# Opening of a two-layer hybrid backbone: all token loads in quarters, eight raw buffers, and the first key and query products queued behind the modulation blocks

## The chip, the cores and the metric

The kernel runs on one core of one Trainium2 chip. The metric is device time in microseconds of one execution of the whole program. Before the change three runs took 1936.62, 1938.57 and 1939.97 us; the median is 1938.57 us.

## The reference

Two consecutive layers of a bidirectional network on 256 latent tokens and 256 context tokens of width 1024, in float32. Only its opening matters here:

```
h_lat, h_ctx = x, ctx
ml = split(silu(c)     @ ada_w[l] + ada_b[l], 6)      # modulation of the latent tokens
mc = split(silu(c_ctx) @ ada_w[l] + ada_b[l], 6)      # modulation of the context tokens
xl = rmsnorm(h_lat, g) * (1 + ml[1]) + ml[0]
xc = rmsnorm(h_ctx, g) * (1 + mc[1]) + mc[0]
yl, yc = even_mixer(xl, xc, ...)                      # begins with xs @ w_in: keys, queries, values, gates
```

After the mixer come a dense SwiGLU, a second mixer and a mixture of eight experts.

## The kernel before, in words

Tokens lie transposed: `res` holds 128 partitions by 8 slabs `k` of 128 channels by 512 tokens (context first). Each float32 product is made of three: weights and tokens are split into a rounded part `hi` and a rest `lo`, and `mm3` (L232) adds hi by hi, hi by lo and lo by hi into one accumulator bank. ScalarE writes the `hi` parts and VectorE the `lo` parts (`hilo`, L634).

The opening, in `even_mixer` from L491 on, does four things.

1. `first_rstd` (L362) loads the tokens in two transfers, squares the eight slabs on ScalarE (L369), adds them on VectorE (L371), sums over partitions on TensorE (L374), takes the reciprocal root with small VectorE steps (L380 to L390) and spreads it over the partitions on TensorE (L398).
2. The modulation comes in blocks of 256 columns. A call of `ada` (L279) loads one block of 1 MB into a raw buffer, multiplies it on TensorE in eight matmuls of 32 by 256 (L286), copies the result to SBUF on VectorE (L289), turns it by two small matmuls (L292) and adds the bias on VectorE (L295). Blocks go in pairs, a scale block into bank `c0` and a shift block into bank `c1`; pair `j` serves the slabs 2j and 2j+1. "Turned" below means that L295 of a pair's second block has run.
3. For each slab VectorE scales the tokens (L506, tile `xm`), ScalarE applies the pair's scale and shift (L405, two instructions per slab, one for each half of the tokens), and `hilo` writes `xhi` and `xlo`.
4. The first products, of the key and query columns of `w_in`, run over the slabs into four banks at once (two called `mm`, one `pr`, one `o`): 3 matmuls of 128 by 512 for each bank and slab, 12 for a slab, 96 in all. Their two weight chunks are loaded in two transfers and split in halves of four slabs.

After them come the gate products (L667), the convolution of the four banks (`conv`, L437) and the delta rule.

Each engine executes its instructions in the order in which they stand, and each may wait on semaphores of the other engines. That order is set by the framework's list scheduler, which sees the whole program and starts from the order in which the code emits. Loads go through SyncE's one queue. Buffers of a pool are reused in turn, and a new load waits until the old content has been read. The raw pool of the opening has six buffers and the eight blocks pass through it; the weight chunks use a ring of their own with two.

Of the kernel before, what the change touches and what calls it, by code (L numbers as in the profile page):

```python
# [18 lines left out]
P = 128  # L19
D = 1024  # L20
KD = 8
# [141 lines left out]
class Kernel:  # L163
# [115 lines left out]
    def ada(self, l, blocks, tag, pool=None):  # L279
        nc = self.nc  # L280
        for b2 in blocks:
            w = self.load(self.I["ada"][b2], pool).rearrange("p (k c) -> p k c", k=KD)
            ps = self.bank(tag)
            for k in (0, 2, 4, 6, 1, 3, 5, 7):
                j = k // 2
                nc.tensor.matmul(ps[32 * j:32 * j + 32, :256], lhsT=self.sT[:, k], rhs=w[:, k],  # L286
                                 start=k % 2 == 0, stop=k % 2 == 1, tile_position=(0, 32 * j))
            part = self.small.tile([P, 256], F32, name="part", bufs=2)
            nc.vector.tensor_copy(part, ps[:, :256])  # L289
            pc = ps[:, 256:260]  # L290
            for i in range(2):
                nc.tensor.matmul(pc[:, 2 * i:2 * i + 2], lhsT=part[:, i * P:(i + 1) * P], rhs=self.cb["sel2"],  # L292
                                 start=True, stop=True)
            bias = self.par[f"ada_b{l}"][:, 2 * b2:2 * b2 + 2]
            nc.vector.tensor_tensor(self.vec[l][:, 2 * b2:2 * b2 + 2], pc.rearrange("p (i r) -> p i r", i=2),  # L295
                                    bias[:, :, None].to_broadcast([P, 2, 2]), op=ALU.add)
# [65 lines left out]
    def first_rstd(self, pool, tag, row):  # L362
        nc = self.nc
        acc = pool.tile([P, T], F32, name="sqacc")
        for i in range(2):
            nc.sync.dma_start(self.res[:, 4 * i:4 * i + 4], self.I["x"][:, 4 * i:4 * i + 4])
        for k in range(KD):
            sq = pool.tile([P, T], F32, tag="sq", name="sq", bufs=3) if k else acc
            nc.scalar.activation(sq, self.res[:, k], AF.Square)  # L369
            if k:  # L370
                nc.vector.tensor_tensor(acc, acc, sq, op=ALU.add)  # L371
        ps = self.bank(tag)
        for t in range(4):
            nc.tensor.matmul(ps[:, t:t + 1], lhsT=acc[:, t * P:t * P + P], rhs=self.mean_d[:, 0:1], start=True,  # L374
                             stop=True)
        return self.rstd_row(self.rstd_col(ps, 4), row)
# [80 lines left out]
    def even_mixer(self):  # L457
        nc, I = self.nc, self.I
        with ExitStack() as st:
# [27 lines left out]
            with ExitStack() as s1:  # L487
                xp = s1.enter_context(self.pool("x0"))
                x = self.pair(xp, "x")
                self.psum(s1, "ps_even", mm=2, pr0=1, pr1=1, c0=1, c1=1, o0=1, o1=1)  # L490
                with ExitStack() as s0:  # L491
                    raw = s0.enter_context(self.pool("raw0", 6))
                    wp = s0.enter_context(self.pool("work0"))
                    vecs = self.mod_vectors(0, 0)
                    banks = [self.bank(t) for t in ("mm", "mm", "pr1", "o1")]
                    rs = self.first_rstd(wp, "o0", "pr0")
                    ahead = []
                    for j in range(4):
                        for i in range(2):
                            self.ada(0, (4 + j - 4 * i,), f"c{i}", raw)  # L500
                            if j < 2 and i:
                                ahead.append(self.weights(I["w_in"][6 - 2 * j], KD))
                        self.mod_scale(vecs[0], 0, 0, slice(2 * j, 2 * j + 2))
                        for k in (2 * j, 2 * j + 1):
                            xm = wp.tile([P, T], F32, tag="xm", name="xm", bufs=3)
                            nc.vector.tensor_tensor(xm, self.res[:, k], rs, op=ALU.mult)  # L506
                            self.modulate_split(xm, k, vecs, x)
                        for k in ((), range(4), (4, 5), (6, 7))[j]:
                            for i, ps in enumerate(banks):
                                m = slice(i % 2 * P, i % 2 * P + P)  # L510
                                whi, wlo = ahead[i // 2]
                                self.mm3(ps, whi(k)[:, m], wlo(k)[:, m], x[0][:, k], x[1][:, k], k == 0, k == KD - 1)
# [80 lines left out]
            with ExitStack() as s3:  # L593
# [4 lines left out]
                raw = s3.enter_context(self.pool("raw1", 2))  # L598
# [1130 lines left out]
```

## Time and profile before

| | |
|---|---|
| median of three runs | 1938.57 us (1936.62 to 1939.97) |
| the profiled execution | 1935.74 us |
| its span, first to last instruction | 1933.9 us |
| granted TensorE clock, mean | 0.967 |
| busy: TensorE, VectorE, ScalarE | 91%, 75%, 52% of the span |

The profile is of one execution. Its span is 1.84 us shorter than its time, which is what lies around the first and last instruction, and its time is 2.83 us below the median. Times inside the trace count from the span's start. In rows of the timeline the first number is the start, the second how long the row lasts (several instructions merged), and the bracket says how long the engine had stood idle and what ended that. The granted clock is shown as a share of full speed: 1.00 is 2.4 GHz, 0.50 is 1.2 GHz. Before the first record of the clock, at 29.8 us, the column shows 1.00 whatever the clock was.

### The profile page before, as it was taken

To read this page: it belongs to the slowest core of one execution; us is meant where nothing else is said; L and a number is where in the kernel's file an instruction comes from. 1 tells how busy PE (TensorE), PEld (TensorE's weight loads), DVE (VectorE), ACT (ScalarE), POOL (GpSimd) and SP (SyncE) were. 2 spreads that over 40 slices of the span, in tenths; PEclk is the share of its full clock that TensorE was granted. 3 is DMA by queue.
4 is the path that set the end of the run, shared out by engine and by line. 5 is a ranking of instruction groups with operands and counts; after the bars stand their busy time and mean duration, and the time that the engine had idled before them with its cause. 6 is when DMAs were issued, how large, how long until landed. Compare 5 with 4: busy or idle time off the path is not lost.

```text
span 1933.9 us, 28843 instructions
## 1 busy us (share of the span) xinstructions
PE 1768.6 (91%) x11628; PEld 1390.4 (72%) x11628; DVE 1445.9 (75%) x1966; ACT 1006.3 (52%) x1131; POOL 90.3 (5%) x92
## 2 busy tenths in 40 slices
PE   6989999698999999989999879989999899998996
PEld 3657776377888888778876768777777677777775
DVE  4577888657995383456685678888888889888987
ACT  3433325635232222366562357776677677767774
POOL 0011102200000000002110000000000000000000
PEclk8999999798999999989999889999999999999997
DMA  7232111325666163123203339999999999989993
GB/s 291 91 111 88 46 42 49 109 88 200 236 238 239 66 223 125 66 80 109 87 23 146 144 133 359 363 344 363 345 341 363 353 346 341 370 335 360 352 380 119
DMA packets 57310, 409.32 MB, mean 212 GB/s; under 512 B 6480, under 2 KB 6864, under 8 KB 8016
## 3 DMA queue, kind: packets, MB, share of 16 engines
q1 hardware_dynamic: 57168, 407.39, 56.5%
q8 instruction: 93, 1.52, 0.3%
q14 instruction: 49, 0.40, 0.1%
HBM read 406.32 MB, written 1.05 MB: 211 GB/s over the span
## 4 chain that ended last, share of the span: by engine, by line
PE 71%; DVE 17%; ACT 7%; issue 4%; POOL 1%; DMA 0%; SPq 0%; DVEq 0%; ACTq 0%; POOLq 0%
DVE lo L636 10%; PE bank_gu L1604 6%; PE bank_b L234 6%; PE bank_b L235 6%; PE bank_b L236 6%; PE bank_gu L1603 5%; ACT hi L635 5%; PE bank_mm L234 4%; PE bank_mm L235 4%; PE bank_mm L236 4%; PE bank_gu L1606 3%; PE bank_dn L1660 3%; PE bank_dn L1659 2%; PE bank_dn L1662 1%; PE bank_tr L1619 1%
## 5 line engine op out<-in xcount | busy, mean ns | idle before, releaser
L636 DVE TENSOR_TENSOR lo<-raw,hi 128x2048 fp32r<-128x2048 f32 (+1 forms) x398 | 765.4, 1946 | 186.3 <-ACT hi L635 184.2
L635 ACT ACTIVATE hi<-raw 128x2048 fp32r<-128x2048 f32 (+1 forms) x398 | 641.3, 1632 | 276.0 <-PE bank_b L235 140.5
L1604 PE MATMUL bank_gu<-lo,xghi 128*128 128x512 f32 (+1 forms) x384 | 148.9, 388 | 27.2 <-DVE lo L636 26.7
L1604 PE MATMUL bank_gu<-lo,xs 128*128 128x512 f32 (+1 forms) x384 | 146.2, 387 | 7.5 <-DVE lo L636 6.4
L1603 PE MATMUL bank_gu<-hi,xghi 128*128 128x512 f32 (+1 forms) x384 | 145.6, 379 | 0.0
L1606 PE MATMUL bank_gu<-hi,xglo 128*128 128x512 f32 (+1 forms) x384 | 144.5, 376 | 0.0
L1603 PE MATMUL bank_gu<-hi,xs 128*128 128x512 f32 (+1 forms) x384 | 144.3, 382 | 0.2
L234 PE MATMUL bank_b<-xhi,hi 128*128 128x512 f32 x352 | 138.0, 394 | 2.9 <-ACT xhi L635 2.9
L234 PE MATMUL bank_mm<-xhi,hi 128*128 128x512 f32 (+1 forms) x320 | 120.9, 380 | 21.5 <-ACT hi L635 15.3
L235 PE MATMUL bank_b<-xlo,hi 128*128 128x512 f32 x352 | 137.9, 392 | 0.0
L236 PE MATMUL bank_b<-xhi,lo 128*128 128x512 f32 x352 | 137.6, 391 | 0.0
L236 PE MATMUL bank_mm<-xhi,lo 128*128 128x512 f32 (+1 forms) x320 | 118.3, 370 | 2.9 <-DVE lo L636 2.1
L235 PE MATMUL bank_mm<-xlo,hi 128*128 128x512 f32 (+1 forms) x320 | 119.7, 374 | 0.0
L1604 PEld LDWEIGHTS bank_gu<-lo,xghi 128*128 128x128 f32 x384 | 72.2, 188 | 54.0 <-DVE lo L636 41.6
L1604 PEld LDWEIGHTS bank_gu<-lo,xs 128*128 128x128 f32 x384 | 72.4, 188 | 32.6 <-DVE lo L636 21.2
L312 DVE SCALAR_TENSOR_TENSOR ada<-ada_raw,sT,ada 128x1024 f32<-128x1024 f32 x70 | 87.2, 1282 | 5.5 <-DMA ada_raw<-in_ada_v 4.8
L234 PEld LDWEIGHTS bank_mm<-xhi,hi 128*128 128x128 f32 x320 | 62.4, 196 | 37.2 <-ACT hi L635 16.5
L1603 PEld LDWEIGHTS bank_gu<-hi,xghi 128*128 128x128 f32 x384 | 72.3, 188 | 13.5
L1603 PEld LDWEIGHTS bank_gu<-hi,xs 128*128 128x128 f32 x384 | 72.4, 188 | 12.4 <-ACT hi L635 1.5
L1606 PEld LDWEIGHTS bank_gu<-hi,xglo 128*128 128x128 f32 x384 | 72.4, 188 | 12.2
L234 PEld LDWEIGHTS bank_b<-xhi,hi 128*128 128x128 f32 x352 | 66.5, 189 | 17.0 <-ACT xhi L635 3.2
L1660 PE MATMUL bank_dn<-lo,hT 128*128 128x512 f32 x176 | 72.8, 414 | 6.2 <-DVE lo L636 6.2
(512 smaller groups left out, 3461.0 us busy)
## 6 DMA issues: line engine op xcount, KB each, us to landing
raw<-in_m_up SPq DMA_DIRECT2D x88, 1024.0 KB, 7.2
raw<-in_m_gate SPq DMA_DIRECT2D x88, 1024.0 KB, 7.1
raw<-in_m_down SPq DMA_DIRECT2D x88, 1024.0 KB, 7.3
ada_raw<-in_ada_v SPq DMA_DIRECT2D x28, 1024.0 KB, 4.9
raw<-in_ada SPq DMA_DIRECT2D x20, 1024.0 KB, 6.0
raw<-in_o_in SPq DMA_DIRECT2D x16, 1024.0 KB, 4.9
raw<-in_w_in SPq DMA_DIRECT2D x12, 1024.0 KB, 4.9
raw<-in_f_gate SPq DMA_DIRECT2D x11, 1024.0 KB, 5.8
```

The costliest lines, as they stand in the source:

```text
L234: mm(out, lhsT=whi, rhs=xhi, start=start, stop=False)
L235: mm(out, lhsT=whi, rhs=xlo, start=False, stop=False)
L236: mm(out, lhsT=wlo, rhs=xhi, start=False, stop=stop)
L312: nc.vector.scalar_tensor_tensor(acc[r], w[:, k], s, acc[r], op0=ALU.mult, op1=ALU.add)
L635: self.nc.scalar.activation(hi, x, AF.Copy)
L636: (self.nc.gpsimd if pool else self.nc.vector).tensor_tensor(lo, x, hi.bitcast(F32), op=ALU.subtract)
L1603: mm(o, lhsT=xg[0][:, kk], rhs=whi(k), start=kk == 0, stop=False)
L1604: mm(o, lhsT=xg[0][:, kk], rhs=wlo(k), start=False, stop=small and kk == 7)
L1606: mm(o, lhsT=xg[1][:, kk], rhs=whi(k), start=False, stop=kk == 7)
L1619: mm(ps[:, 256 * i + 64 * j:256 * i + 64 * j + 64], lhsT=t[:, j * P:(j + 1) * P], rhs=self.cm["sum2"], start=True, stop=True)
L1659: mm(py[a], lhsT=h[0], rhs=whi(i)[:, half[a]], start=f == 0, stop=False)
L1660: mm(py[a], lhsT=h[0], rhs=wlo(i)[:, half[a]], start=False, stop=len(h) == 1 and f == FT - 1)
```

## The change

Four edits, all in the opening. The raw pool has eight buffers in place of six. The tokens come in four transfers of two slabs in place of two of four. The first products leave the loop over pairs and stand in a loop of their own behind it. And each slab's products are emitted under `issue_after`, which adds an edge in TensorE's order: the products of slabs 0 and 1 have to stand behind the last turning matmul (L292) of pair 2, those of the other slabs behind that of pair 3.

```diff
@@ ada
-                nc.tensor.matmul(pc[:, 2 * i:2 * i + 2], lhsT=part[:, i * P:(i + 1) * P], rhs=self.cb["sel2"],
-                                 start=True, stop=True)
+                self.turned = nc.tensor.matmul(pc[:, 2 * i:2 * i + 2], lhsT=part[:, i * P:(i + 1) * P],
+                                               rhs=self.cb["sel2"], start=True, stop=True)
@@ first_rstd
-        for i in range(2):
-            nc.sync.dma_start(self.res[:, 4 * i:4 * i + 4], self.I["x"][:, 4 * i:4 * i + 4])
+        for i in range(4):
+            nc.sync.dma_start(self.res[:, 2 * i:2 * i + 2], self.I["x"][:, 2 * i:2 * i + 2])
@@ even_mixer
-                    raw = s0.enter_context(self.pool("raw0", 6))
+                    raw = s0.enter_context(self.pool("raw0", 8))
...
-                    ahead = []
+                    ahead, turned = [], []
...
-                        for k in ((), range(4), (4, 5), (6, 7))[j]:
+                        turned.append(self.turned)
+                    for k in range(KD):
+                        with self.tc.issue_after(turned[2 if k < 2 else 3].ins):
                             for i, ps in enumerate(banks):
```

Lines from the two new ones on count two higher in the changed kernel (L636 is L638 there, L667 is L669).

On TensorE, where the second pair of blocks stands (tiles 261 and 277 in banks `c0` and `c1`), the program before has the first products (L234 to L236) between the blocks and right behind them:

```order
L286 MATMUL bank_c0_261<-raw_259,sT_74 32x256 x8
L235 MATMUL bank_mm_159<-xlo_148,hi_306 128x512
L236 MATMUL bank_mm_159<-xhi_147,lo_307 128x512
L292 MATMUL bank_c0_261<-const_base_60,part_270 128x2 x2
L286 MATMUL bank_c1_277<-raw_275,sT_74 32x256 x8
L234 MATMUL bank_mm_160<-xhi_147,hi_306 128x512
L235 MATMUL bank_mm_160<-xlo_148,hi_306 128x512
L236 MATMUL bank_mm_160<-xhi_147,lo_307 128x512
L292 MATMUL bank_c1_277<-const_base_60,part_286 128x2 x2
L234 MATMUL bank_mm_159<-xhi_147,hi_306 128x512
```

In the changed program the second pair (263 and 279) and the third (310 and 326) stand there without a product, and the first product follows the last turning of the third pair:

```order
L286 MATMUL bank_c0_263<-raw_261,sT_74 32x256 x8
L292 MATMUL bank_c0_263<-const_base_60,part_272 128x2 x2
L286 MATMUL bank_c1_279<-raw_277,sT_74 32x256 x8
L292 MATMUL bank_c1_279<-const_base_60,part_288 128x2 x2
L286 MATMUL bank_c0_310<-raw_308,sT_74 32x256 x8
L286 MATMUL bank_c1_326<-raw_324,sT_74 32x256
L292 MATMUL bank_c0_310<-const_base_60,part_319 128x2 x2
L286 MATMUL bank_c1_326<-raw_324,sT_74 32x256 x7
L292 MATMUL bank_c1_326<-const_base_60,part_335 128x2 x2
L234 MATMUL bank_mm_159<-xhi_147,hi_398 128x512
```

So 48 products that stood ahead of the third pair stand behind it, and the fourth pair's matmuls, which stood behind those 48 as well, now stand among the first 20.

On VectorE, from the end of the second pair on, the program before has this; the copy of the third pair's first block (364) is the last row:

```order
L295 TENSOR_TENSOR vec0_72<-bank_c1_277,par_58 128x4
L636 TENSOR_TENSOR xlo_148<-xm_294,xhi_147 128x512
L506 TENSOR_TENSOR xm_401<-res_71,bank_pr0_207 128x512
L636 TENSOR_TENSOR lo_317<-raw_291,hi_316 128x1024
L636 TENSOR_TENSOR xlo_148<-xm_300,xhi_147 128x512
L636 TENSOR_TENSOR lo_408<-raw_244,hi_407 128x1024
L506 TENSOR_TENSOR xm_472<-res_71,bank_pr0_207 128x512
L636 TENSOR_TENSOR lo_418<-raw_291,hi_417 128x1024
L289 COPY part_373<-bank_c0_364 128x256
```

The changed program has at the same place (the third pair's first block is 310 there):

```order
L295 TENSOR_TENSOR vec0_72<-bank_c1_279,par_58 128x4
L638 TENSOR_TENSOR xlo_148<-xm_296,xhi_147 128x512
L506 TENSOR_TENSOR xm_347<-res_71,bank_pr0_209 128x512
L638 TENSOR_TENSOR lo_409<-raw_293,hi_408 128x1024
L638 TENSOR_TENSOR xlo_148<-xm_302,xhi_147 128x512
L638 TENSOR_TENSOR lo_455<-raw_246,hi_454 128x1024
L506 TENSOR_TENSOR xm_386<-res_71,bank_pr0_209 128x512
L289 COPY part_319<-bank_c0_310 128x256
```

The last `lo` has left; the six instructions between the end of the second pair and the copy of the third have stayed. A pair earlier the sequence gains one: the first half chunk's `lo_399` (with `hi_398` on ScalarE) now stands between the first pair's two slabs, where `lo_307` had been made ahead of them. Behind the opening the five engines' orders are the same as before.

## Rows read from the trace of the kernel before

**Rows 1.** The page's chain of waits, shares of the span by engine.
```profile
PE 71%; DVE 17%; ACT 7%; issue 4%; POOL 1%; DMA 0%; SPq 0%; DVEq 0%; ACTq 0%; POOLq 0%
```

**Rows 2.** Busy time by stretch: PE, PEld, DVE, ACT, POOL, granted clock, DMA share, GB/s.
```profile
29.80:30.00 0.20, 0.00 (x0) 0.00 (x0) 0.03 (x1) 0.20 (x1) 0.00 (x0) 0.52 1.27 532
...
43.40:43.60 0.20, 0.20 (x2) 0.13 (x2) 0.20 (x1) 0.20 (x1) 0.00 (x0) 0.85 0.00 0
```

**Rows 3.** Timeline, from the sums of squares to the first pair turned.
```profile
11.36 5.47 DVE L371 TENSOR_TENSOR sqacc<-sqacc,sq 128x512 f32<-128x512 f32 x7 [1.11 <-ACT sq L369]
...
16.89 1.87 PE L374 MATMUL bank_o<-mean_d,sqacc 128*128 128x1 f32 x8 [0.59 <-DVE sqacc L371]
...
18.80 0.16 DVE L390 TENSOR_SCALAR mcol<-bank_o 128x4 f32<-128x4 f32 x1 [1.96 <-PE bank_o L374]
...
19.78 0.16 DVE L383 SCALAR_TENSOR_TENSOR newton<-rcol,mcol 128x4 f32<-128x4 f32 x1
...
21.15 1.01 PE L292 MATMUL bank_c<-const_base,part 128*128 128x2 f32 x4 [0.54 <-DVE part L289]
...
23.10 2.08 PE L398 MATMUL bank_pr<-const_base,rcol 128*128 128x128 f32 x8
...
25.10 1.67 PE L286 MATMUL bank_c<-raw,sT 128*32 128x256 f32 x10
...
27.94 0.16 DVE L295 TENSOR_TENSOR vec<-bank_c,par 128x4 f32<-128x4 f32 x1
```

**Rows 4.** Timeline, the second pair and the parts that stand beside it.
```profile
28.13 1.58 ACT L405 ACTIVATE xm<-xm,vec,gs 128x256 f32<-128x256 f32 x3 [6.95 <-DVE vec L295]
...
33.02 0.42 DVE L289 COPY part<-bank_c 128x256 f32<-128x256 f32 x1
...
34.67 1.93 PE L286 MATMUL bank_c<-raw,sT 128*32 128x256 f32 x16
...
38.87 0.16 DVE L295 TENSOR_TENSOR vec<-bank_c,par 128x4 f32<-128x4 f32 x1 [1.77 <-PE bank_c L292]
...
41.57 1.04 ACT L635 ACTIVATE hi<-raw 128x1024 fp32r<-128x1024 f32 x1
...
42.65 1.22 DVE L636 TENSOR_TENSOR lo<-raw,hi 128x1024 fp32r<-128x1024 f32 x1
```

**Rows 5.** Timeline of VectorE behind the second pair.
```profile
45.52 0.68 DVE L506 TENSOR_TENSOR xm<-res,bank_pr 128x512 f32<-128x512 f32 x1
```

**Rows 6.** Timeline of TensorE: products, a turning, the first gate product.
```profile
36.54 0.80 PE L234 MATMUL bank_mm<-xhi,hi 128*128 128x512 f32 x1
...
58.23 0.61 PE L292 MATMUL bank_c<-const_base,part 128*128 128x2 f32 x4 [0.54 <-DVE part L289]
...
61.66 0.39 PE L234 MATMUL bank_mm<-xhi,hi 128*128 128x512 f32 x1
...
69.83 0.40 PE L236 MATMUL bank_o<-xhi,lo 128*128 128x512 f32 x1
...
70.06 0.39 PE L667 MATMUL bank_c<-xhi,gatew 128*32 128x512 f32 x1
```

**Rows 7.** Loads: SyncE's issues, then size and us from issue to landing.
```profile
2.14 0.91 SPq L366 DMA_DIRECT2D res<-in_x  x2
10.17 16.96 SPq L214 DMA_DIRECT2D raw<-in_ada  x4
```

**Rows 8.** Loads one by one: size, us from issue to landing.
```profile
res<-in_x SPq DMA_DIRECT2D x1, 1024.0 KB, 8.0
...
res<-in_x SPq DMA_DIRECT2D x1, 1024.0 KB, 10.0
...
raw<-in_ada SPq DMA_DIRECT2D x1, 1024.0 KB, 19.9
...
raw<-in_w_in SPq DMA_DIRECT2D x1, 1024.0 KB, 4.9
...
gw<-in_gate_w SPq DMA_DIRECT2D x1, 512.0 KB, 3.5
```

## Prediction

> **What bounds the kernel now.** I read the page's chain of waits first: TensorE holds 71% of it, VectorE 17%, DMA nothing [rows 1]. The change touches only the first 70 of 1934 us, so the rest was read in the timeline of that stretch, engine by engine, with the granted clock and the loads beside it. The reader is to see there that the opening is one chain: loads, root of the mean square, pairs of blocks turned one after the other, products. TensorE has something to do in almost all of it from 30 us on, half of that time at the 1.2 GHz level: the clock falls at 29.8 and rises at 43.4 us [rows 2]. The last product starts at 69.83 and the first gate product at 70.06 us [rows 6]. Everything behind it keeps its order on all five engines, and at that point only the products are being waited for. So I measure the change by one number, E, the start of the first gate product, 70.06 us now, and carry its shift to the end unshortened.
>
> Three moments on the way are read in the trace before: the first pair is turned at 27.94 us (V0) [rows 3], the second at 38.87 (V1) [rows 4], and between and behind them TensorE does products, from 36.54 us on without pause [rows 6].
>
> **The change, part by part.**
>
> *Raw buffers, eight for six.* The last two blocks no longer wait for a free buffer. A block's load issued early takes 19.9 us to land because it stands in a full queue [rows 8]; the fifth to the eighth block are issued from 10.17 to 27.1 us [rows 7]. The fifth thus lands at 30.1, and the others follow by about the 2.5 us that part the landings of two transfers of 1 MB in a full queue (2.14 plus 8.0 and some 2.6 plus 10.0 us [rows 7, 8]): 32.6, 35 and 37.6. Nothing in the changed order could use any of them before 39 us (below), so the edit is worth 0.
>
> *Tokens in quarters.* ScalarE can begin half a transfer's step earlier, 1.25 us. VectorE's seven adds take 5.47 us [rows 3], 0.78 each, and depend on one another, and in the new order five small steps of the decay constants stand between them. Bounds: 0 and minus 1.25; I take minus 0.7, so the sums on TensorE (L374) start at 16.2 instead of 16.89. An own price per transfer is a rival below.
>
> *First pair.* In the changed order L374 stands ahead of all blocks, and the root runs unbroken: 16.2 plus 1.87 for L374, eleven small steps at 0.196 (five from 18.80 to 19.78) make 2.15, 0.3 to TensorE, 2.08 for L398: 22.6 [rows 3]. It was 25.2. But in the meantime TensorE has done only three block matmuls, which is all that the new order puts there; it stands waiting behind L374's result. Behind L398 come the other five of the first block and five of the second (1.67 for five: 3.3), the first turning (1.01), three matmuls (about 1.0), a copy and its hand-over (0.5), the second turning (0.61 to 1.01) [rows 3, 6]: V0 = 22.6 + 6.6 = 29.2 at the low clock. The clock before had a high stretch just ahead of 29.8 us, in which a turning took less; I take V0 = 28.9, bounds 27.9 and 29.5.
>
> *Second pair.* Before, the copy of its first block ran at 33.02, 5.08 us behind V0 [rows 3, 4]. The same VectorE instructions still stand ahead of it, and one more pair is now in the chain: the half chunk's `hi` on ScalarE (1.04) and `lo` on VectorE (1.22) [rows 4], which were made earlier, beside waiting. Because the two engines overlap, that adds some 1.2: copy at V0 + 6.3. Then hand-over 0.5, turning 1.0, the second block's eight matmuls 1.93 [rows 4], copy and hand-over 0.55, turning 0.9: V1 = V0 + 11.2 at the low clock, 10 at the high one. I take 11.0, so V1 = 39.9. Before it took 10.9 with six products in between, which have gone; the wait is VectorE's queue, not TensorE.
>
> *Third pair: the added wait.* Products must now stand behind its second turning. Its first block's matmuls are done soon after V1, but on VectorE the copy stands behind six instructions: two `xlo`, two `lo` and two `xm` of the second pair and the weights. They need ScalarE's work that begins at V1. Before, the same six ended their issue at 45.52 plus 0.6 for the last, 7.25 us behind V1 [rows 4, 5], and nobody noticed, because TensorE had 36 products to do there. Now TensorE has one matmul and then nothing. Copy at V1 + 7.25, then hand-over 0.5, turning 1.0, seven matmuls 1.7, copy and hand-over 0.55, turning 0.8: 11.8 (12.2 all at the low clock, 10.6 at the high one). First product at P0 = 39.9 + 11.8 = 51.7 us. Queued behind the waiting turning are all 96 products; before, 48 of them stood ahead of the third pair.
>
> *Products.* From 61.66 to 69.83 lie 35 steps, 0.2335 each [rows 6]: 96 make 22.4 at 2.4 GHz. The fourth pair now stands among the first 20. Its matmuls are 1.93 at the low clock, so about 1.0 to 1.1 at the high, a turning 0.61 [rows 4, 6]: 2 x 1.7 = 3.4. Its copies have five and three products as cover; if that is gone, 0.5 each. TensorE comes to P0 from waiting, so at 1.2 GHz. Before, the rise at 43.4 came 6.9 us behind 36.54, from where on TensorE was never idle [rows 2, 6]. Half of such a stretch is lost: 3.4. I take 3.0, bounds 2.4 and 7.0 (the clock stays low through the mixed part too, some 14 us). Sum 28.8, E = 51.7 + 28.8 = 80.5.
>
> *Elsewhere.* The second weight halves need buffers that come free 12 products ahead of their use (2.8 us) and take 1.04 plus 1.22 [rows 4]: hidden, with little to spare. Later loads start relative to the work, not to the clock on the wall: 0.
>
> **Sum.** E moves from 70.06 to 80.5, plus 10.4 us. On the profiled execution, 1935.74 us (span 1933.9 and 1.84 around it), that makes 1946.1. The median lies 2.83 above that execution, so 1949.0 beside it; I go to 1948, a little inside, since the three overlaps that I priced at the low clock may meet a high one.
>
> **Rivals.**
>
> *The blocks turn as they land (faster).* If VectorE's queue did not hold the copies, the third pair would be turned soon after its second load, 32.6 us: eight matmuls 1.93, copy 0.5, turning 0.9 and hand-overs, P0 = 36.3 and E = 36.3 + 28.8 = 65.1, 5 us less: 1933.6. For it speaks that before, the last turning ran at 58.23 us [rows 6] though the last block's load had been issued by 27.1 [rows 7]. Against it speaks that VectorE's rows follow the written order, and that order puts the copy last. The point from which it decides is P0 below 41.3.
>
> *It is given back (no change).* The change loses its 10 us and later stages take them up, for instance loads that are further ahead when the products end. Against it: DMA has 0% of the chain [rows 1]. Price: 1938.6, give or take 3.
>
> *The quarters cost (slower still).* In a full queue two transfers of x land 2.5 us apart, while one alone takes 4.9 and half of one 3.5 [rows 8]: the fixed part is paid beside the transfer ahead. If each transfer paid for itself, four of 3.5 against two of 4.9 would add 4.2 us to the root, to V0 and to all behind: E = 84.7, 1952.
>
> The Trainium skill speaks for this rival: "DMA: Bandwidth & Descriptors", section Bandwidth, says to batch transfers to 1 MiB or more, since below that a fixed cost weighs. By that rule this case would come out at the 1952 above; the landings 2.5 us apart disagree with it here, since the queue is full at that point.
>
> **How the numbers follow.** The forecast has 0.79, the quarters' price 0.05 more on the same side; the blocks turning as they land 0.08; given back, or a shift that my sum overstates so far that under 4 us are left, 0.08. This kernel's measurement can tell about 0.2%, 3.9 us, from no change. Slower 0.84, same 0.08, faster 0.08. The forecast's own range: P0 between 49 and 53 with the losses of 2.4 to 7 gives E from 76.8 to 86, 1944 to 1954 on the median. Low end to 1940 to take in part of the smaller shifts.
>
> **What would show it.** L374 earlier by some 0.7 us, L398 by 2 to 3; V0 near 29 and V1 near 40; TensorE idle between about 41 and 47, released by the copy (L289); the copy right behind an `xm` (L506); first product at about 51.7 at 1.2 GHz and the rise 5 to 7 us later; the first gate product (L669) near 80.5, and the distance from it to the end as before, 1863.8 us, within 2. I am wrong if the first product stands before 42, or if the tail behind the gate products has become shorter.

## The result and the profile after

The change makes the kernel slower. In the first comparison four executions had a median of 1954.45 us (1952.79 to 1956.72) against 1938.41 for the kernel before, a ratio of 1.0082 [1.0068, 1.0095]; the forecast was 1948, 1940 to 1954. The profiled execution took 1954.51 us, its span 1952.6 us. Two more sets gave 1.0079 [1.0053, 1.0105] and 1.0058 [1.0036, 1.0079]. Over all executions, 19 of the changed kernel and 105 of the one before, the means are 1952.3 and 1938.7 us: 13.6 us apart, give or take 1.7 (1.96 standard errors, from deviations of 3.7 and 2.8 us in single executions).

The chain of waits has 70% for TensorE, 18% for VectorE and still nothing for DMA [rows 1]:

```profile
PE 70%; DVE 18%; ACT 7%; issue 4%; POOL 1%; DMA 0%; SPq 0%; DVEq 0%; ACTq 0%; POOLq 0%
```

The second trace of the kernel before has the same shares, so the step from 71 to 70% says nothing on the change. TensorE's timeline after, from the sums of squares to the first gate product, answers to [rows 3, 4, 6]:

```profile
17.26 1.84 PE L374 MATMUL bank_o<-mean_d,sqacc 128*128 128x1 f32 x8 [17.26 <-DVE sqacc L371]
...
21.32 2.08 PE L398 MATMUL bank_pr<-const_base,rcol 128*128 128x128 f32 x8 [1.23 <-DVE rcol L385]
...
36.35 1.01 PE L292 MATMUL bank_c<-const_base,part 128*128 128x2 f32 x4 [4.88 <-DVE part L289]
...
48.55 1.02 PE L292 MATMUL bank_c<-const_base,part 128*128 128x2 f32 x4 [5.06 <-DVE part L289]
...
52.83 0.77 PE L234 MATMUL bank_mm<-xhi,hi 128*128 128x512 f32 x1
...
57.96 0.57 PE L235 MATMUL bank_pr<-xlo,hi 128*128 128x512 f32 x1
58.37 0.39 PE L236 MATMUL bank_pr<-xhi,lo 128*128 128x512 f32 x1
...
80.98 0.39 PE L669 MATMUL bank_c<-xhi,gatew 128*32 128x512 f32 x1
```

In the two rows with 4.88 and 5.06 in the bracket TensorE stands still until VectorE has copied a block (L289). The second of them is the change. Before, 42 products filled that place, and the copy waited for TensorE:

```profile
51.97 0.42 DVE L289 COPY part<-bank_c 128x256 f32<-128x256 f32 x1 [0.35 <-PE bank_c L286]
```

The first of the two costs little: from the first pair turned to the second it is 11.19 us after and was 10.93 before [rows 3, 4]. The first product comes at 52.83 us. The row's length tells the clock: 0.57 to 0.77 us per product at first, 0.39 from 58.37 on (starts 0.42 to 0.43 us apart, then 0.23).

VectorE's timeline after, from the second block of the first pair, shows why the copy is late; it answers to [rows 4, 5]:

```profile
29.64 0.16 DVE L295 TENSOR_TENSOR vec<-bank_c,par 128x4 f32<-128x4 f32 x1 [0.44 <-PE bank_c L292]
...
40.83 0.16 DVE L295 TENSOR_TENSOR vec<-bank_c,par 128x4 f32<-128x4 f32 x1 [1.11 <-PE bank_c L292]
43.16 0.69 DVE L638 TENSOR_TENSOR xlo<-xm,xhi 128x512 fp32r<-128x512 f32 x1 [2.17 <-ACT xhi L637]
43.89 0.69 DVE L506 TENSOR_TENSOR xm<-res,bank_pr 128x512 f32<-128x512 f32 x1
44.60 1.23 DVE L638 TENSOR_TENSOR lo<-raw,hi 128x1024 fp32r<-128x1024 f32 x1
45.74 0.68 DVE L638 TENSOR_TENSOR xlo<-xm,xhi 128x512 fp32r<-128x512 f32 x1
46.34 1.22 DVE L638 TENSOR_TENSOR lo<-raw,hi 128x1024 fp32r<-128x1024 f32 x1
47.48 0.68 DVE L506 TENSOR_TENSOR xm<-res,bank_pr 128x512 f32<-128x512 f32 x1
48.08 0.42 DVE L289 COPY part<-bank_c 128x256 f32<-128x256 f32 x1
```

The first of the six waits 2.17 us for ScalarE, the others follow without a gap, and the copy stands behind them, 7.25 us behind the second pair's turning, to the hundredth what the forecast took from [rows 4, 5].

SyncE's issues after show the earlier loads [rows 7]: the last four blocks no longer wait for a buffer, and the last is issued by 19.2 us in place of 27.1.

```profile
2.14 2.09 SPq L366 DMA_DIRECT2D res<-in_x  x4
...
12.62 6.57 SPq L214 DMA_DIRECT2D raw<-in_ada  x4
```

### The profile page after: what moved, and what is told of

The parts are those of the page before. It is cut to its first block, busy times and chain, and to the rows that moved or that the text cites. A ratio compares the mean times of both kernels' runs of the same rounds, so it can differ in the third digit from the quotient of the medians.

```text
span 1952.6 us, 28846 instructions
## 1 busy us (share of the span) xinstructions
PE 1776.0 (91%) x11628; PEld 1395.9 (71%) x11628; DVE 1445.4 (74%) x1966; ACT 1006.5 (52%) x1131; POOL 88.8 (5%) x92
## 4 chain that ended last, share of the span: by engine, by line
PE 70%; DVE 18%; ACT 7%; issue 4%; POOL 1%; DMA 0%; SPq 0%; DVEq 0%; ACTq 0%; POOLq 0%
DVE lo L638 10%; PE bank_gu L1606 6%; PE bank_b L234 6%; PE bank_b L235 6%; PE bank_b L236 6%; PE bank_gu L1605 5%; ACT hi L637 5%; PE bank_mm L234 4%; PE bank_mm L236 4%; PE bank_mm L235 4%; PE bank_gu L1608 3%; PE bank_dn L1662 3%; PE bank_dn L1661 2%; PE bank_dn L1664 1%; PE bank_tr L1621 1%
## 5 line engine op out<-in xcount | busy, mean ns | idle before, releaser
L638 DVE TENSOR_TENSOR lo<-raw,hi 128x2048 fp32r<-128x2048 f32 (+1 forms) x398 | 765.4, 1946 | 189.3 <-ACT hi L637 187.1
L1606 PE MATMUL bank_gu<-lo,xghi 128*128 128x512 f32 (+1 forms) x384 | 149.6, 389 | 27.1 <-DVE lo L638 26.7
L234 PE MATMUL bank_b<-xhi,hi 128*128 128x512 f32 x352 | 138.0, 394 | 2.9 <-ACT xhi L637 2.9
L234 PE MATMUL bank_mm<-xhi,hi 128*128 128x512 f32 (+1 forms) x320 | 121.1, 380 | 19.3 <-ACT hi L637 15.4
L236 PE MATMUL bank_b<-xhi,lo 128*128 128x512 f32 x352 | 137.5, 391 | 0.0
L236 PE MATMUL bank_mm<-xhi,lo 128*128 128x512 f32 (+1 forms) x320 | 118.3, 370 | 2.1 <-DVE lo L638 2.1
L234 PEld LDWEIGHTS bank_mm<-xhi,hi 128*128 128x128 f32 x320 | 63.0, 197 | 33.6 <-ACT hi L637 16.7
L1605 PEld LDWEIGHTS bank_gu<-hi,xghi 128*128 128x128 f32 x384 | 72.7, 189 | 13.6
L234 PEld LDWEIGHTS bank_b<-xhi,hi 128*128 128x128 f32 x352 | 66.5, 189 | 16.9 <-ACT xhi L637 3.2
```

What stands on the lines that cost most here:

```text
L234: mm(out, lhsT=whi, rhs=xhi, start=start, stop=False)
L236: mm(out, lhsT=wlo, rhs=xhi, start=False, stop=stop)
L638: (self.nc.gpsimd if pool else self.nc.vector).tensor_tensor(lo, x, hi.bitcast(F32), op=ALU.subtract)
L1605: mm(o, lhsT=xg[0][:, kk], rhs=whi(k), start=kk == 0, stop=False)
L1606: mm(o, lhsT=xg[0][:, kk], rhs=wlo(k), start=False, stop=small and kk == 7)
```

## The experiments

All kernels in one table. E is the start of the first gate product in the profiled execution; times are means, ratios are those of the comparison on the same chip.

| kernel | executions | mean us | ratio to before | E |
|---|---|---|---|---|
| before | 105 | 1938.7 | 1.0001 [0.9987, 1.0016] (against itself) | 69.2 (mean of 4) |
| changed | 19 | 1952.3 | 1.0082, 1.0079, 1.0058 (above) | 79.7 (mean of 6) |
| moved and held products alone | 5 | 1948.5 | 1.0060 [1.0047, 1.0073] | 78.6 |
| loads alone | 12 | 1942.6 | 1.0023 [1.0011, 1.0036] | 70.2 |
| changed, not held | 12 | 1939.3 | 1.0010 [0.9998, 1.0023] | 66.6 |
| changed, copies one pair earlier | 12 | 1945.7 | 1.0032 [1.0019, 1.0046] | 76.9 |
| changed, three pairs' copies first | 5 | 1945.2 | 1.0038 [1.0023, 1.0052] | 73.2 |
| before, token loads held up | 12 | 1939.7 | 1.0005 [0.9993, 1.0018] | 70.4 |
| own loop, not held, old loads | 12 | 1939.0 | 1.0004 [0.9989, 1.0019] | 66.7 |
| the same, first pair ahead of the tokens | 12 | 1935.4 | 0.9986 [0.9977, 0.9996] | 63.5 |

E stands in one execution only, and the clock makes it vary from one to the next. In three of the four traces of the kernel before, the first product with a row of about 0.39 us, that is at the full clock, stands at 42.8 to 43.5 us and E at 69.3 to 70.1; in the second trace it stands at 36.42, and E at 67.8. From the first trace, then from the second:

```profile
43.51 0.40 PE L236 MATMUL bank_mm<-xhi,lo 128*128 128x512 f32 x1
...
36.42 0.39 PE L235 MATMUL bank_mm<-xlo,hi 128*128 128x512 f32 x1
```

The single traces of the loads alone, of the two loops not held and of the last kernel have it early as well, at 34.6 to 38.8 us. Beside the 67.8 of the early trace their E are 2.4 us later, 1.3 and 1.1 earlier and 4.4 earlier, which is nearer to what their times show than the distance from the mean of 69.2. How often each kernel has the early rise is open.

### The change taken apart

**Moved and held products, with the old buffers and loads** (edit of the changed kernel).

```diff
-        for i in range(4):
-            nc.sync.dma_start(self.res[:, 2 * i:2 * i + 2], self.I["x"][:, 2 * i:2 * i + 2])
+        for i in range(2):
+            nc.sync.dma_start(self.res[:, 4 * i:4 * i + 4], self.I["x"][:, 4 * i:4 * i + 4])
...
-                    raw = s0.enter_context(self.pool("raw0", 8))
+                    raw = s0.enter_context(self.pool("raw0", 6))
```

> The moved and held products alone, with six buffers and two token transfers as before. Theory A (the products behind the third pair cost what was lost): the first pair is turned as before near 27.9, the second near 38 to 39, the copy of the third pair stands 7.25 us behind that, first product at 49.5 to 51, first gate product at 78 to 80 us, 8 to 10 us behind the kernel before in the opening; with up to 5 us more behind it the time is 1946 to 1955 us. Theory B (the early order of the first pair, or the quarters and buffers, carry a good part): less than 4 us behind before, 1938 to 1942 us.

Measured: pairs turned at 28.51 and 38.44 us, first product at 50.45, E at 78.6, median 1948.4. Theory A, in every number: the products' place carries most of the loss.

**Loads alone**: eight buffers and four token transfers, put into the kernel before (the same lines, the other way round).

> Eight buffers and four token transfers alone; the products stand between the blocks as before. Theory A (buffers and quarters are worth next to nothing; what they move is only the order of the first pair): first pair turned at 29 to 30 us in place of 27.9, first gate product at 68 to 72 us, time within 3 us of before. Theory B (the early loads or the first pair's new order carry a good part of the loss): first gate product at 74 us or later, 5 us or more behind before.

Measured: first pair turned at 28.99, E at 70.2, but a ratio of 1.0023, 4.5 us [2.1, 7.0]. E falls in theory A's bounds, the time is a little above them. TensorE's timeline shows a later start. Before, the first product stood at 30.29 us:

```profile
30.29 0.80 PE L234 MATMUL bank_mm<-xhi,hi 128*128 128x512 f32 x1 [2.39 <-ACT xhi L635]
```

With the loads alone it stands at 32.78, and there is a wait more:

```profile
32.78 0.80 PE L234 MATMUL bank_mm<-xhi,hi 128*128 128x512 f32 x1 [3.83 <-ACT hi L635]
...
42.17 0.73 PE L234 MATMUL bank_mm<-xhi,hi 128*128 128x512 f32 x2 [1.11 <-ACT xhi L635]
```

The sums now stand ahead of all blocks, and the first product waits for the first weights' `hi`, which ScalarE makes late. That E hardly shows these 2.5 us agrees with the clock, which rose early in this trace (first product at the full clock at 38.82 us); it is also the shortest of the twelve executions, 1937.07 us. So the later start is shown, and that it makes up the whole 3.8 us is not. The two parts, 9.8 and 3.8 us on the means (1948.54 and 1942.56 less 1938.72), add up to the 13.6 of both; by the ratios they are 11.6 and 4.5, which the intervals allow as well.

**The hold taken away**, everything else as in the change.

```diff
-                        with self.tc.issue_after(turned[2 if k < 2 else 3].ins):
+                        if True:
```

> The changed kernel without the edge that holds the products: eight buffers, four token transfers, products emitted in a loop of their own, but free to stand between the blocks. Theory A (the hold costs): products begin about 6 us behind the first pair's turning (29.6 us), TensorE has them as work while the third and fourth pair go through VectorE, and the first gate product comes at 64 to 72 us; 1933 to 1942 us. Theory B (the emission behind the blocks, the quarters or the first pair's new order cost by themselves): first gate product at 76 us or later, 1945 us or more.

Measured: E at 66.6, median 1939.7, both in theory A's bounds (the first product came 3.8 us behind the first pair, not 6). A loop of its own costs nothing that shows here, and gains nothing either; the edge costs, because without it the third and fourth pair stand among the products.

### Is it VectorE's queue?

**Copies one pair earlier.** All blocks are emitted first, and each pair's modulation is held, on VectorE, behind the second copy of the next pair.

```diff
+                        copied.append(self.copied)
+                    for j in range(4):
+                        with self.tc.issue_after(copied[min(j + 1, 3)].ins):
...
```

> The changed kernel with the same hold on the products, but on VectorE each pair's two copies stand ahead of the modulation of the pair before it. Theory A (the wait is VectorE's queue: six instructions that need ScalarE stand ahead of the third pair's copy): the third pair's copy stands within 2 us of its matmuls, the first product comes at 41 to 45 us in place of 52.8 and the first gate product at 69 to 75 us; 1937 to 1944 us. Theory B (the hold itself costs, whatever VectorE's order, by the loads or by the clock): first product later than 49 us, first gate product at 78 us or more, 1947 us or more.

Measured: first product at 48.51, E at 76.9, median 1946.0, between the two theories. Its timeline of TensorE tells why:

```profile
36.42 1.01 PE L292 MATMUL bank_c<-const_base,part 128*128 128x2 f32 x4 [0.55 <-DVE part L289]
...
44.20 1.01 PE L292 MATMUL bank_c<-const_base,part 128*128 128x2 f32 x4 [4.91 <-DVE part L289]
```

One of the two long waits has gone, the other stands: the third pair's copy was still behind the first pair's modulation. The edit took away half of what it was meant to.

**Copies of three pairs first.** The same, with `copied[(2, 2, 2, 3)[j]]`.

> The hold as in the change, and on VectorE the copies of the first three pairs ahead of every modulation. In the kernel before this one (copies of a pair ahead of the modulation of the pair before it) one of the two waits of 4.9 us for the copy had gone and one was left, at 44.20 us; its first product came at 48.5 and its first gate product at 76.9. Theory A (each of the two waits is VectorE's queue): no wait of more than 2 us between the turnings is left, the third pair is turned at 43 to 45 us; then the first tokens are only beginning to be scaled, so the first product comes at 44 to 48 us and the first gate product at 72 to 77; 1939 to 1946 us. Theory B (the hold costs by another way, such as the clock): first product at 48.5 us or later, first gate product at 77 or later, 1946 us or more.

TensorE's timeline has its longest wait for a copy and its first product here:

```profile
40.24 1.01 PE L292 MATMUL bank_c<-const_base,part 128*128 128x2 f32 x4 [1.00 <-DVE part L289]
...
46.68 1.22 PE L234 MATMUL bank_mm<-xhi,hi 128*128 128x512 f32 x2
```

That wait is 1.00 us now, the third pair is turned at 44.71, the first product stands at 46.68 and E is 73.2; median 1944.4. All as theory A said, so the two waits were VectorE's queue. But E is still 4 us behind that of the kernel before (69.2). VectorE's timeline has the first scaling of a slab here:

```profile
43.59 0.68 DVE L510 TENSOR_TENSOR xm<-res,bank_pr 128x512 f32<-128x512 f32 x1
```

Before, products ran without pause from 36.54 us [rows 6]; here no slab exists before 43.59. Holding the products costs even where VectorE's order is turned to suit it.

### The tail behind the first gate product

The first pair of traces differed by 10.9 us at E and by 18.7 at the end. Repeated executions were to tell whether those 7.8 us belong to the change.

> The kernel before, executed once more for its trace. Behind the opening the changed kernel's profile was 7.8 us longer than that of before, at places where the granted clock lay at 0.50 in one and not in the other. Theory 'each execution' (the low stretches fall differently from one execution to the next): this trace has its low stretches behind 100 us at other places than the first one (98 to 105, 340 to 351, 821 to 839, 1064 to 1071, 1108 to 1129 us), and the time from the first gate product to the end is somewhere in 1861 to 1872 us. Theory 'the shift' (the shifted start decides where they fall): the same places again, within 3 us, and 1863.8 give or take 1 us from the first gate product to the end.

> The changed kernel, executed once more for its trace. Theory 'each execution': low stretches behind 100 us at other places than in its first trace (109, 181, 280, 355, 409, 464, 836, 1078, 1126, 1321 us), time behind the first gate product anywhere in 1861 to 1872 us. Theory 'the shift': the same places, 1871.6 give or take 1 us behind the first gate product. By both the opening is as in its first trace: first product at 52.8, first gate product at 81.0 us, give or take 0.7.

> The changed kernel again, for more executions. So far its five executions have a mean of 1953.7 us and those of before one of 1937.8: 15.8 apart, while the first gate product came 11.0 to 13.2 us later in the two traces of each. Theory 'each execution' (low-clock stretches fall at random): more executions bring the difference nearer to the opening's 11 to 12 us, 1948 to 1952 us, and in the trace the time behind the first gate product, less half of TensorE's busy time at the low level there, is 1830 to 1833 us again. Theory 'the changed program meets more of them': the difference stays at 15 to 17 us, 1953 to 1955 us.

> The changed kernel's trace once more. Of ten traces so far the time behind the first gate product was 1868.3 to 1871.9 us in the five with held products and 1863.8 to 1868.1 in the five without. Theory 'each execution': it can fall anywhere in 1863 to 1872 us. Theory 'held products bring more low-clock stretches behind them': 1868 us or more again. By both, the time less half of TensorE's busy time at the low level there is 1830 to 1833 us.

> The changed kernel. Time behind the first gate product in its four traces so far: 1871.6, 1868.3, 1868.4, 1871.5; in two of before: 1863.8, 1868.1. Theory 'drawn in each execution': 1863 to 1872 us, and the median over the rounds nearer to 11 us behind before than to 15 (1948 to 1951 us). Theory 'the changed program': 1868 us or more again, 14 to 16 us behind before (1952 to 1955 us).

> The kernel before, against itself. By both theories the ratio is 1 within its interval, which shows what two sets of executions of one program differ by. Behind the first gate product, theory 'drawn in each execution': anywhere in 1863 to 1872 us; theory 'the changed program': 1863 to 1868 us, as its two traces so far.

> The changed kernel's trace once more. Theory 'drawn in each execution': 1863 to 1872 us behind the first gate product. Theory 'the changed program': 1868 us or more.

> The trace of before once more. Theory 'drawn in each execution': 1863 to 1872 us behind the first gate product. Theory 'the changed program': 1868 us or less. By both, the time less half of TensorE's busy time at the low level there is 1828 to 1833 us.

| trace | E | span less E | TensorE busy at 0.50 in it | less half of that |
|---|---|---|---|---|
| before, first | 70.06 | 1863.8 | 64.4 | 1831.6 |
| before, 2 | 67.84 | 1868.1 | 75.4 | 1830.4 |
| before, 3 | 69.34 | 1871.6 | 80.1 | 1831.5 |
| before, 4 | 69.56 | 1871.2 | 84.6 | 1828.9 |
| changed, first | 80.98 | 1871.6 | 79.8 | 1831.7 |
| changed, 2 | 79.79 | 1868.3 | 71.3 | 1832.7 |
| changed, 3 | 80.39 | 1868.4 | 77.0 | 1829.9 |
| changed, 4 | 79.14 | 1871.5 | 84.5 | 1829.2 |
| changed, 5 | 79.26 | 1871.2 | 77.3 | 1832.6 |
| changed, 6 | 78.39 | 1867.6 | 72.1 | 1831.6 |

The fourth column adds up TensorE's busy time over the rows whose granted clock lies below 1.00, by their share at 0.50; a product's step is 0.43 us there against 0.23 (above), so a little under half of it is lost, and without half of it the ten tails agree within 4 us. The tails themselves run from 1863.8 to 1871.6 for one and the same kernel. Four stretches of before's first trace show it (busy time by engine, with granted clock, DMA share and GB/s):

```profile
172.00:176.00 4.00, 4.00 (x47) 3.13 (x47) 4.00 (x6) 3.40 (x8) 2.98 (x2) 1.00 0.00 0
...
1306.00:1312.00 6.00, 6.00 (x28) 4.85 (x27) 5.53 (x4) 3.84 (x2) 0.00 (x0) 1.00 0.95 354
1507.00:1510.00 3.00, 3.00 (x15) 2.36 (x14) 3.00 (x3) 1.92 (x1) 0.00 (x0) 1.00 0.99 374
1708.00:1712.00 4.00, 4.00 (x21) 3.28 (x20) 3.40 (x3) 3.26 (x3) 0.00 (x0) 1.00 0.99 395
```

and the same stretches of its third trace, which ends 7.0 us later (span 1940.9 against 1933.9):

```profile
172.00:176.00 4.00, 4.00 (x28) 3.36 (x27) 3.23 (x5) 3.02 (x7) 2.95 (x2) 0.57 0.00 0
...
1306.00:1312.00 6.00, 5.69 (x13) 4.45 (x14) 4.65 (x3) 0.60 (x1) 0.00 (x0) 0.50 0.82 283
1507.00:1510.00 3.00, 2.78 (x7) 2.20 (x8) 3.00 (x3) 0.00 (x0) 0.00 (x0) 0.50 0.55 167
1708.00:1712.00 4.00, 4.00 (x12) 3.10 (x12) 3.13 (x2) 1.38 (x1) 0.00 (x0) 0.57 0.91 367
```

TensorE is busy nearly throughout in both, and the clock is another. What stands just ahead is the same in both as well: TensorE pauses for 1.9 us ahead of the first of the four stretches and for 2.7 us ahead of the others. The end of the pause ahead of the second stretch, in the first trace and in the third:

```profile
1303.80 0.50 PE L1604 MATMUL bank_gu<-lo,xghi 128*128 128x512 f32 x1 [2.70 <-DVE lo L636]
...
1306.31 0.79 PE L1604 MATMUL bank_gu<-lo,xghi 128*128 128x512 f32 x1 [2.70 <-DVE lo L636]
```

The same program pauses equally long at the same place, and only in the third trace does the clock fall to 0.50 there. The theory 'drawn in each execution' holds for the traces. 'The shift' went with the first repetition: 1868.1 in place of 1863.8 give or take 1, and 1868.3 in place of 1871.6. After two traces of before and four of the changed kernel it still looked like 'the changed program' (1866.0 against 1870.0 on the means), and the third and fourth of before undid that. The means are now 1868.7 and 1869.8, 1.1 apart. The times alone would not have decided it: the changed kernel's second set had a median of 1953.3, inside the other theory's 1953 to 1955, and its third set, at 1951.0, lies on the edge of this one's 1948 to 1951. Of the 13.6 us, E accounts for 10.5 and the tail in the traces for 1.1; the last 2 us are no more than the 1.7 of the means and the spread of so few traces leave open, and stay unexplained. A tail that is longer by up to some 3 us in the changed kernel is not excluded. By the Trainium skill ("TensorE: Matmul & The Clock Gate", Part 1) the clock gate does not start anew with a kernel, so where it switches depends on how the work happens to lie against it; that two traces of one program differ agrees with this, and the 7.8 us that it came to here is from the rows.

### Two kernels that followed from this

**Token loads held up.** The kernel before with five fills of half the token tile on VectorE ahead of the token loads, meant as a plain shift.

```diff
+        for _ in range(5):
+            nc.vector.memset(self.res[:, 0:4], 0.0)
```

> The kernel before with five fills of half the token tile on VectorE ahead of the token loads, which only shift its start. The shift is read at the first gate product. Theory 'each execution': the time is that of before plus this shift, within 2 us, and the time behind the first gate product less half of TensorE's low-clock busy time there is 1830 to 1833 us. Theory 'the shift decides': the time grows by 3 to 6 us more than the shift.

The shift did not come about: E is 70.4, the ratio 1.0005, and it says nothing on the tail. What it shows is of use all the same. The sums stood at 26.29 instead of 16.89 [rows 3], and the products ran on from 37.49 instead of 36.54 [rows 6]. The blocks of the first pair had been loaded and turned by then (19.73 us): what was lost in the root was won in the blocks.

**The loop not held, with six buffers and two token transfers.**

> The products in their own loop but not held, with six buffers and two token transfers as before: the third and fourth pair stand among the products. Theory A (of the change, the loads' part costs 3 to 4 us by the later first pair and the hold the rest; the loop by itself is harmless or useful): first gate product at 64 to 68.5 us, 1933 to 1938.5 us. Theory B (the loop by itself costs, as the kernel with the free loop and the early loads had 1939 us although its first gate product came at 66.6): 1939 us or more.

Measured: E at 66.7 and a median of 1936.9, as theory A said; yet the mean is 1939.0, and the ratio of 1.0004 cannot be told from none, since five of its twelve executions lie at 1941.8 to 1946.0.

**The same, with the first pair of blocks emitted ahead of the token loads.**

```diff
+                    for i in range(2):
+                        self.ada(0, (4 - 4 * i,), f"c{i}", raw)
                     rs = self.first_rstd(wp, "o0", "pr0")
...
-                            self.ada(0, (4 + j - 4 * i,), f"c{i}", raw)
+                            if j:
+                                self.ada(0, (4 + j - 4 * i,), f"c{i}", raw)
```

> As the free loop with six buffers, and the first pair of blocks is emitted ahead of the tokens' loads and their mean square. In the run with fills the token loads were held up so that the sums (L374 there L376) stood at 26.3 in place of 16.9 us, yet the second pair was turned at 36.9 and the first gate product stood at 70.4. Theory A (the first pair's blocks can go ahead of the root for nothing, and the root then is followed by the second pair at once): first pair turned at 17 to 22 us, sums at 20 to 24 us, second pair at 32 to 36, first gate product at 62 to 67; 1931 to 1937 us. Theory B (the root of the tokens is the longer chain): second pair turned at 37 us or later, first gate product at 68 us or more, 1938 us or more.

TensorE's timeline in it:

```profile
10.01 1.93 PE L286 MATMUL bank_c<-raw,sT 128*32 128x256 f32 x16 [10.01 <-DMA raw<-in_ada]
...
15.90 1.02 PE L292 MATMUL bank_c<-const_base,part 128*128 128x2 f32 x4 [0.55 <-DVE part L289]
22.55 1.86 PE L374 MATMUL bank_o<-mean_d,sqacc 128*128 128x1 f32 x8 [5.63 <-DVE sqacc L371]
...
27.66 2.08 PE L398 MATMUL bank_pr<-const_base,rcol 128*128 128x128 f32 x8 [2.25 <-DVE rcol L385]
...
33.24 0.50 PE L234 MATMUL bank_mm<-xhi,hi 128*128 128x512 f32 x1
...
63.46 0.40 PE L672 MATMUL bank_c<-xhi,gatew 128*32 128x512 f32 x1
```

Every number lies in theory A's bounds but the first pair, which is turned at 16.96, just ahead of the 17. This pair is done before the tokens are needed, products start at 33.24 and run on, and E is 63.5. The ratio is 0.9986 [0.9977, 0.9996], 2.7 us faster than the kernel before [0.8, 4.5]: the only version here that is faster than the kernel before. Against the same loop without this order, on the same chip, the mean is 3.6 us lower and E 3.2 us earlier; the early rise of the clock in this trace has some part in E.

## Why the prediction was right and where it was not

- *Buffers, worth 0.* The last four blocks are issued from 12.62 us, and TensorE waits for no block's load in the opening of the first trace. The buffers were not tried without the quarters; the two together cost 3.8 us on the means, and what the trace shows of it is the first product 2.5 us later.
- *Tokens in quarters, minus 0.7.* Wrong, if small. ScalarE's first square starts at 10.08 us, and started at 10.18: the first quarter landed 7.9 us after its issue, the first half before 8.0. L374 came at 17.26, later than the 16.89 before, in the first trace, and 0.2 later on the means (17.0 of six traces, 16.9 of four). A price did appear, at the other end: the last quarter was issued at 3.6 us and landed 10.3 us behind that, at 13.9; the last half was issued at 2.6 and landed 10.0 behind that, at 12.6 [rows 8]. The first and the last quarter:

```profile
res<-in_x SPq DMA_DIRECT2D x1, 512.0 KB, 7.9
...
res<-in_x SPq DMA_DIRECT2D x1, 512.0 KB, 10.3
```

That is 1.3 us and not the 4.2 of the third rival; how much of the 0.4 at L374 comes from it is open.
- *First and second pair.* V0 was to be 28.9 and is 29.64 (27.4 to 29.6 in six traces, mean 28.5); V1 was to be 39.9 and is 40.83 (mean 39.6). Between them lie 11.19 us in the first trace, the low-clock sum of 11.2.
- *The added wait.* Copy at V1 + 7.25, as said (7.24 or 7.25 in all six traces); P0 51.7 forecast, 52.83 in the first trace, 51.6 in the mean of six. The blocks did not turn as they landed. The kernel with three pairs' copies first shows that VectorE's queue was the reason. The products that hid the same queue before were 42, not 36; no term hangs on that.
- *Products.* From P0 to E the forecast had 28.8; 28.15 in the first trace. In all six traces the first product at the full clock stands 5.2 to 5.5 us behind P0, as the 5 to 7 forecast. (From 30 us to E before, a third of the time was at the 1.2 GHz level, 13.6 of 40 us by [rows 2], not half.) The second trace of the changed kernel has clock records there that show the low stretch and its end behind the first products:

```profile
33.00:45.00 12.00, 6.59 (x42) 3.38 (x42) 5.95 (x12) 5.01 (x8) 0.14 (x2) 0.50 0.32 131
45.00:56.00 11.00, 8.03 (x41) 5.07 (x45) 3.98 (x9) 3.22 (x6) 0.00 (x0) 0.50 0.41 149
57.00:58.00 1.00, 1.00 (x5) 0.82 (x6) 1.00 (x3) 0.00 (x0) 0.00 (x0) 1.00 0.00 0
```

- *Sum.* E moved by 10.9 us in the first pair of traces, 10.5 on the means; forecast 10.4. That it fits so closely is partly luck: on the means E after is 0.8 us earlier than forecast (79.7 for 80.5), and E before 0.9 earlier than the one read (69.2 for 70.06). Given back (the second rival) was nothing. By its own terms the range of E starts at 77.2 (49 + 22.4 + 3.4 + 2.4), not at 76.8.
- *The step that failed* is the one behind E: "I measure the change by one number, E [...] and carry its shift to the end unshortened", with the distance from E to the end "as before, 1863.8 us, within 2". That distance had been read in one execution, the shortest of ten. It is 1871.6 in the first trace after, 1869.8 on the mean of six, and for the kernel before itself anywhere from 1863.8 to 1871.6. With the forecast's own E of 80.5, the mean tail of ten traces (1869.3) and the 1.84 around the span, the sum would have been 1951.6 us, next to the measured mean of 1952.3. The same sum for the kernel before, with its mean E of 69.2, gives 1940.3 where 1938.7 was measured, so some 2 us of the shift stay open by it. The median's 2.83 above the profiled execution had already said that this execution was short; added to the sum, it made up for a part. The one step back from 1949.0 to 1948, for overlaps at a high clock, went the wrong way, and the range up to 1954 held only the opening's uncertainty: no term stood for the spread of single executions, 3.7 us here. The first four drew a median of 1954.45, 2.1 above the mean of all and 0.45 beyond the range; the mean of 1952.3 lies inside it.

## What to carry to other kernels

When work that covered a wait is moved behind it, price the wait by what stands in the helper engine's queue ahead of the awaited instruction: here six VectorE instructions, 7.25 us, were visible in the trace before and came out to the hundredth. A moment in an opening moves by some 2 us with the clock from one execution to the next, so compare traces with the same rise. Before a tail is called rigid, set its length against a second trace or the spread of the runs, and correct its busy time by the granted clock; a difference of one pair of profiles is no better than that spread. And an opening's loads can be ordered by which chain can run alone: here the first pair's blocks could, and with the tokens' sums 5.6 us later than in the same loop without that order (22.55 for 16.94) the kernel was 3.6 us faster.

## What the runs showed that was not expected

- One and the same program loses some 30 to 40 us of its tail to the low clock (a little under half of 64.4 to 84.6 us of TensorE's busy time), depending on the execution. Behind one and the same pause of 1.9 or 2.7 us the clock falls in one execution and stays at 1.00 in another.
- Four token transfers of 512 KB brought the first data no sooner than two of 1 MB: 7.9 against 8.0 us from issue to landing for the first in the first traces (7.3 to 8.1 in the six of the changed kernel, 7.7 to 8.1 in the four of before), in a queue that had other transfers ahead; the last data came 1.3 us later.
- Token loads held back until the sums stood 9.4 us later moved the first gate product by 1.2 us against the mean of before (70.4 against 69.2), within that kernel's own 67.8 to 70.1 but for 0.3.
